# Four of eleven weight sums moved from the up projections to the first projections of a hybrid encoder block

## The chip, the cores and the metric

The kernel runs on one core of one Trainium2 chip. The metric is the device time of one execution in microseconds; lower is better. The core's engines are TensorE (PE, its weight loads PEld), VectorE (DVE), ScalarE (ACT), GpSimd (POOL) and SyncE (SP, which here only issues DMAs).

## The reference

One encoder block for 512 tokens of width 1024, all in float32:

```python
h = rms_norm(x, mix_norm_g)
proj = h @ w_in                      # mLSTM q,k,v,o,gates | NA q,k,v | memory q | merge gates
y_ml = mlstm_branch(...)             # bidirectional, chunkwise
y_na = neighbourhood_attention(...)  # 8 heads, 8 x 16 windows with bias
y_xa = memory_cross_attention(...)   # into rms_norm(mem)
merged = g_ml * (y_ml @ w_br_ml) + g_na * (y_na @ w_br_na) + g_xa * (y_xa @ w_br_xa)
x = x + merged @ w_out
a, u = split(rms_norm(x, ffn_norm_g) @ w_ffn_up)           # 1024 -> 2 x 2816
x = x + (gelu(dwconv3(a, w_conv, b_conv)) * u) @ w_ffn_down  # 2816 -> 1024
return rms_norm(x, final_norm_g)
```

The change concerns `w_ffn_down` (2816 x 1024) alone.

## The kernel before, in words

*Arithmetic.* A float32 product is made as three matmuls of rounded parts (`mm3`, lines 224 to 226): high x high, high x low, low x high. Each operand is therefore split: ACT writes the high part with a copy that rounds (line 184 for weights, 230 for activations), DVE subtracts it from the source for the low part (185, 231).

*Weights.* The weights of all projections lie in one array of blocks in the order of use (`BLOCKS`): four blocks `mlq`, four `mlk`, eight `tm` (values and gates, token-major), then `xaq`, `o`, `memk`, `memv`, `naq`, `nak`, gates and branches, and last 22 pairs `ua`, `uu` of the up projections. `weights(key)` is called where a block is first needed. It starts the DMA of blocks up to three ahead (`emit_raw`, line 160, on SP's queue, three buffers) and the split of the next one (`emit_split`, in halves, four buffers each for high and low parts). `BINDEX` gives a block's number; `mlk` 0 is 4, `xaq` 0 is 16.

*The down projection* is done by a Winograd-like scheme: its input and its weight are cut into 2 x 2 quarters, and seven products of sums of quarters (`ORDER`: p1, p5, p6, p3, p7, p2, p4) take the place of eight. The sums of the weight's quarters are made ahead of time, tile by tile (11 tiles of 128 rows, `HF`), and stored to DRAM: `tdn` holds two plain sums, `tsp` two sums already split into high and low. One tile is one sum of this text:

- `sum_load(k)`: 1 MB of the four quarters from `wdn` into a shared buffer (`unit`), DMA on POOL's queue (line 1477)
- first step: DVE adds two pairs of quarters (1495)
- `high`: takes a second shared buffer, DVE adds (1483), ACT writes the high parts (1484)
- `store`: DVE adds (1492), POOL issues the store to `tdn` (1493)
- `low`: DVE writes the low parts (1487), POOL issues two stores to `tsp` (1489)

The steps stand in the list `down_sums`, in the order first step, `high`, `store`, `low`. In the up projections, loop variable f from 0 to 21, iteration f loads the sum that `SUMS` names for it, and from f = 4 on takes up to three steps from the list:

```python
SUMS = [2 + 4 * k // 3 for k in range(HF)]
...
        if f in SUMS:
            sum_load(SUMS.index(f))
        if f >= 4:
            for _ in range(3):
                if down_sums:
                    down_sums.pop(0)()
```

*Order and buffers.* The program is traced in this order and then list-scheduled: on each engine and queue an instruction that is ready goes first by its place in the trace, with readiness as estimated at compile time. On the chip each engine works its list in order. `tc.issue_after(ins)` keeps instructions behind `ins` on the engine of `ins`. `unit` is a pool of 15 buffers of 128 x 2112 words, shared by operands, activations, heads' work and the sums.

*The first projections.* For `mlq`, eight steps over the input's k tiles are made with four banks at once, while x still arrives. `mlk` 0 and 1 follow, with two banks of another pool, begun earlier. During `mlk` 0 the token norm is made (`x_norm`: `rstd_wide`, lines 347 to 351, gives `rb_x`; `rstd_cols`, 337 and 340, gives `rc_x`). Then the convolutions evacuate the six banks (line 468 multiplies a bank by `rb_x` into `pad`, 470 to 472 convolve, 476 is the SiLU). `mlk` 2 needs the first of the four `mlq` banks back. The `tm` blocks follow; line 538 stores values to `nav_d` through POOL's queue.

Of the kernel before, what the change touches and what calls it, by code (L numbers as in the profile page):

```python
# [11 lines left out]
F32 = mybir.dt.float32  # L12
F32R = mybir.dt.float32r
AF = mybir.ActivationFunctionType
ALU = mybir.AluOpType
# [3 lines left out]
S = 512  # L19
# [6 lines left out]
HF = FT // 2  # L26
# [63 lines left out]
BINDEX = {}  # L90
# [12 lines left out]
def hybrid_block(ctx, tc, xg, xT, xtok, memT, wflat, wout, wdn, vecs, gbias, nabias, out):  # L103
    nc = tc.nc
    V, A, G, PE, SY = nc.vector, nc.scalar, nc.gpsimd, nc.tensor, nc.sync
# [13 lines left out]
    def nm(s):  # L119
        uid[0] += 1  # L120
        return f"{s}_{uid[0]}"

    def unit(dt=F32):
        return up.tile([P, UNIT], dt, tag="unit", name=nm("u"))
# [15 lines left out]
    B11, B12, B22, B21 = range(4)  # L140
    T1, T4, T3, T2 = range(4)
    GROUPS = ((0, 4), (4, 8), (8, HF))
    tdn = dp.tile([2, P, HF * S], F32, name="tdn")
    tsp = dp.tile([2, 2, P, HF * S], F32R, name="tsp")
# [4 lines left out]
    st = {"raw": 0, "split": 0, "last": BINDEX[("ua", 0)][0] - 1}  # L149

    def emit_raw(i):
        key, n = BLOCKS[i]
        _, off, _ = BINDEX[key]
        r = wp.tile([P, BW], F32, tag="raw", name=nm("wr"), bufs=3)
        raws[i] = r
        if i < 2:
            return [(r[:, a:b], wflat[off + P * a:off + P * b].rearrange("(p n) -> p n", p=P))
                    for a, b in zip(CUTS[i], CUTS[i][1:])]
        src = wflat[off:off + P * n].rearrange("(p n) -> p n", p=P)
        st["sy"] = SY.dma_start(r[:, :n], src).ins  # L160
# [7 lines left out]
    def emit_split(i):  # L168
        key, n = BLOCKS[i]
        r = raws.pop(i)  # L170
        c, hs = halves(i)
        split[i] = []
        for a, b in hs:
            m = (b - a) * c
            h = wp.tile([P, HWT], F32R, tag="hi", name=nm("wh"), bufs=4)
            l = wp.tile([P, HWT], F32R, tag="lo", name=nm("wl"), bufs=4)
            if key[:2] == ("tm", 2):
                h = h[:, HI256:]
            for u, v in ((0, P), (P, 2 * P), (2 * P, m)) if i == 0 and a == 0 else ((0, m),):
                src = r[:, a * c + u:a * c + v]  # L180
                if i == 0 and u == 0:
                    st["wh1"] = V.tensor_copy(h[:, u:v], src).ins
                else:
                    A.activation(h[:, u:v], src, AF.Copy)  # L184
                V.tensor_tensor(l[:, u:v], src, h[:, u:v].bitcast(F32), op=ALU.subtract)  # L185
            for k in range(a, b):
                q = slice((k - a) * c, (k - a + 1) * c)
                split[i].append((h[:, q], l[:, q]))
# [4 lines left out]
    def ahead_to(raw, spl):  # L193

        while st["raw"] <= min(raw, st["last"]):
            emit_raw(st["raw"])
            st["raw"] += 1
        while st["split"] <= min(spl, st["last"]):
            emit_split(st["split"])
            st["split"] += 1  # L200

    def weights(key):

        i, _, n = BINDEX[key]
        calls[0] += i >= BINDEX[("naq", 0)][0]
        if calls[0] % 2 and sums:
            sums.pop(0)()
        ahead_to(i + RAW_AHEAD, i + SPLIT_AHEAD)
        return split.pop(i)

    def sum_ops():
        for dst, src, more in ((T1, wout[B11], B12), (T3, wout[B12], B22), (T2, tout[T1], B22), (T4, tout[T2], B21)):
            for add in (False, True):
                def one(d=tout[dst], s=wout[more] if add else src, add=add):
                    if add:
                        G.dma_start(d, s, accum_op=ALU.add, max_dma_last_dim=4 * KT // 2 * S)
                    else:
                        with tc.issue_after(st["sy"]):
                            SY.dma_start(d, s)

                yield one

    def mm3(ps, lh, ll, rh, rl, start, stop):
        PE.matmul(ps, lh, rh, start=start, stop=False)  # L224
        PE.matmul(ps, lh, rl, start=False, stop=False)  # L225
        st["mm"] = PE.matmul(ps, ll, rh, start=False, stop=stop).ins  # L226
# [178 lines left out]
    def proj(key, XHs, XLs, n=S, at={}, ps=None):  # L405

        ws = weights(key)
        k0 = 0 if ps is None else 1
        if ps is None:
            ps = mmps()  # L410
        for k in range(k0, KT):
            mm3(ps[:, :n], ws[k][0], ws[k][1], XHs[k], XLs[k], k == 0, k == KT - 1)
            if k in (1, 3, 5):
                flush()
            if k in at:
                at[k]()
        return ps
# [3 lines left out]
    for k in range(KT):  # L421
        if k % 2 == 0:
            ws = weights(("mlq", k // 2))
        while done < min(KT, k + 1 + (k > 2)):
            x_part(done)
            done += 1
        wh, wl = ws[k % 2]
        if k == 1:

            for w, x in ((wh, XH), (wh, XL), (wl, XH)):  # L430
                for f in range(4):
                    PE.matmul(ps_q[f], w[:, f * P:(f + 1) * P], x[1], start=False, stop=False)  # L432
            continue
        for f in range(4):
            fs = slice(f * P, (f + 1) * P)
            if k == 0 and f == 0:
                hs = (slice(0, S // 2), slice(S // 2, S))
                for h in hs:
                    x_low(h)
                for i, (w, x, j) in enumerate(((wh, XH, 0), (wl, XH, 0), (wh, XH, 1), (wl, XH, 1), (wh, XL, 0), (wh, XL, 1))):  # L440
                    PE.matmul(ps_q[0][:, hs[j]], w[:, fs], x[0][:, hs[j]], start=i == 0, stop=False)
                continue
            mm3(ps_q[f], wh[:, fs], wl[:, fs], XH[k], XL[k], k == 0, k == KT - 1)
        if k == 0:
            ku = unit(F32R)
            kh, kl = ku[:, :2 * P], ku[:, S:S + 2 * P]
            split_act(kh, kl, wk)
            for f in range(2):
                fs = slice(f * P, (f + 1) * P)
                mm3(ps_k[f], kh[:, fs], kl[:, fs], XH[0], XL[0], True, False)  # L450
# [59 lines left out]
    for c in range(3):  # L510
        n, nk = TMC[c], TMK[c]
# [730 lines left out]

    gens = []
    so_ = list(sum_ops())
    sums.extend([so_[0], so_[2], so_[1], so_[3]] + so_[4:])

# [60 lines left out]
    for f in range(4):  # L1307
        ps = paced(("naq", f), RN)
        V.tensor_tensor(nq[:, f * S:(f + 1) * S].rearrange("p (b r c) -> p b r c", r=ROWS, b=4), rv(ps), rv(rb),
                        op=ALU.mult)  # L1310
# [15 lines left out]
    for br in range(3):  # L1326
# [19 lines left out]
        for fp in range(4):  # L1346
# [16 lines left out]
            for i in range(2):  # L1363
                f = 2 * fp + i
                ps = mmps()
                for k in range(4):
                    ks, fs = slice(k * S, (k + 1) * S), slice(i * P, (i + 1) * P)
# [71 lines left out]
    for n, name in enumerate(ORDER_O):  # L1439
        obank[name] = wide()  # L1440
        for k in range(4):
# [18 lines left out]
            for t in range(2):  # L1460
                q = slice(k * HS + t * P, k * HS + (t + 1) * P)
# [5 lines left out]
    for t in range(2):  # L1467
        normed(2 + t)


    down_sums = []

    def sum_load(k):
        w = unit()[:, :4 * S]
        w4 = w.rearrange("p (q n) -> p q n", q=4)
        ks = slice(k * S, (k + 1) * S)
        G.dma_start(w4, wdn[:, :, ks].rearrange("q p n -> p q n"))
        q = [w[:, i * S:(i + 1) * S] for i in range(4)]
        hl = []

        def high():
            hl.append(unit(F32R)[:, :4 * S].rearrange("p (x q n) -> p x q n", x=2, q=2))
            V.tensor_tensor(q[B22], q[B22], q[B11], op=ALU.add)
            A.activation(hl[0][:, 0], w4[:, 1:3], AF.Copy)  # L1484

        def low():
            V.tensor_tensor(hl[0][:, 1], w4[:, 1:3], hl[0][:, 0].bitcast(F32), op=ALU.subtract)
            for x in range(2):
                G.dma_start(tsp[:, x, :, ks].rearrange("q p n -> p q n"), hl[0][:, x])  # L1489

        def store():
            V.tensor_tensor(q[B21], q[B21], q[B22], op=ALU.add)
            G.dma_start(tdn[:, :, ks].rearrange("q p n -> p q n"), w4[:, 0:4:3])

        down_sums.extend([lambda: V.tensor_tensor(w[:, :2 * S], w[:, S:3 * S], w[:, :2 * S], op=ALU.add), high, store, low])


    PRODUCTS = {"p1": (wdn, B11), "p5": (tdn, 0), "p6": (tsp, 1), "p3": (wdn, B22), "p7": (tsp, 0), "p2": (wdn, B21),
                "p4": (tdn, 1)}
    TILES = [(n, k) for n in ORDER for k in range(HF)]  # L1500
# [51 lines left out]
            ops[name, g] = operand(name, quarters(g), GROUPS[g][1] - GROUPS[g][0])  # L1552
            ahead["op"] += 1

    SUMS = [2 + 4 * k // 3 for k in range(HF)]
    for f in range(FT):
        i, j = divmod(f, HF)
        if j % 4 == 0:
# [22 lines left out]
        V.tensor_tensor(ur, pu, c, op=ALU.mult)  # L1581
# [3 lines that stand above are left out]
# [76 lines left out]
    x = xt[3]  # L1661
# [137 lines left out]
```

## Time and profile before

| | |
|---|---|
| median of 3 runs | 857.08 us (856.96 to 857.18) |
| the profiled execution's own time | 857.81 us |
| its span, first to last instruction | 856.0 us |
| mean granted TensorE clock | 0.998 |
| TensorE busy | 848.5 us, 4175 matmuls |
| first projections (`mlk` 0 to the last `tm`) | about 28 to 94 us of the span |
| up projections | about 500 to 740 us |
| sums: first load issued, last store issued | 504.8 us, 690.0 us |

The profile is of one execution. A matmul's row lasts longer than the distance to the next matmul's start, as matmuls overlap; so the count of matmuls in a stretch says more of TensorE's pace than the busy time does. In a group's row, "out<-in" are the program's names; in a timeline row, the bracket is the idle time of the engine just before it and what ended it; PEq, SPq and so on are the engines' sequencers.

### The profile page before, as it was taken

How to read it: one execution, taken by the hardware profiler on the slowest of the kernel's cores; microseconds unless marked ns; L12 is line 12 of the kernel's file. 1: busy time of each engine (PE TensorE's matmuls, PEld its weight loads, DVE VectorE, ACT ScalarE, POOL GpSimd, SP SyncE). 2: the span in 40 equal slices, each digit the busy share in tenths (PEclk: the TensorE clock that was granted, in tenths of full speed). 3: DMA queues.
4: the chain of work that ended last, by engine and by line, in shares of the span. 5: the costliest groups of instructions: out<-in, count | busy, mean ns of one | idle time of the engine just before them, and what ended most of it. 6: DMA issues, size and time to landing. Idle time of an engine off the chain costs nothing.

```text
span 856.0 us, 12111 instructions
## 1 busy us (share of the span) xinstructions
PE 848.5 (99%) x4175; PEld 717.3 (84%) x4175; DVE 622.5 (73%) x1277; ACT 481.2 (56%) x989; POOL 133.0 (16%) x245
## 2 busy tenths in 40 slices
PE   9999999999999999999999999999999999999996
PEld 7898889988888888888888888888888888888885
DVE  7774698987568758898769967475758666694684
ACT  7663467675446658888735764343444444463463
POOL 0101100010127561600000111030213100011101
PEclk9999999999999999999999999999999999999999
DMA  7233542495674444543452844487869672477942
GB/s 281 80 111 121 185 153 85 158 281 163 179 202 120 115 125 127 158 144 128 144 186 98 225 144 156 153 293 261 265 222 348 208 231 99 135 258 258 380 161 100
DMA packets 53982, 155.00 MB, mean 181 GB/s; under 512 B 6872, under 2 KB 11992, under 8 KB 53344
## 3 DMA queue, kind: packets, MB, share of 16 engines
q1 hardware_dynamic: 30912, 101.37, 34.5%
q0 software_dynamic: 22576, 52.46, 20.8%
q8 instruction: 33, 0.54, 0.3%
q10 hardware_dynamic: 432, 0.39, 0.1%
q14 instruction: 29, 0.24, 0.1%
HBM read 132.68 MB, written 29.90 MB: 190 GB/s over the span
## 4 chain that ended last, share of the span: by engine, by line
PE 99%; DVE 0%; ACT 0%; POOLq 0%; issue 0%
PE mm L224 25%; PE mm L225 25%; PE mm L226 25%; PE at L225 6%; PE at L224 6%; PE at L226 6%; PE at L990 1%; PE at L971 1%; PE at L952 0%; PE at L953 0%; PE at L773 0%; PE at L821 0%; PE at L1078 0%; PE at L253 0%; PE mm L432 0%; PE mm L846 0%
## 5 line engine op out<-in xcount | busy, mean ns | idle before, releaser
L224 PE MATMUL mm<-u,wh 128*128 128x512 f32 (+1 forms) x859 | 330.2, 385 | 0.1
L225 PE MATMUL mm<-u,wh 128*128 128x512 f32 (+1 forms) x859 | 327.8, 382 | 0.0
L226 PE MATMUL mm<-u,wl 128*128 128x512 f32 (+1 forms) x859 | 327.7, 382 | 0.0
L184 ACT ACTIVATE wh<-wr 128x512 fp32r<-128x512 f32 (+2 forms) x240 | 149.7, 628 | 233.9 <-PE mm L225 199.8
L185 DVE TENSOR_TENSOR wl<-wr,wh 128x512 fp32r<-128x512 f32 (+2 forms) x242 | 164.1, 683 | 85.5 <-ACT wh L184 85.0
L226 PEld LDWEIGHTS mm<-u,wl 128*128 128x128 f32 x859 | 161.4, 188 | 31.5
L225 PEld LDWEIGHTS mm<-u,wh 128*128 128x128 f32 x859 | 161.6, 188 | 30.3 <-DVE u L231 0.4
L224 PEld LDWEIGHTS mm<-u,wh 128*128 128x128 f32 x859 | 161.4, 188 | 30.2 <-ACT u L230 0.4
L548 POOL DMA_DIRECT2D u<-nav_d x128 | 62.8, 534 | 56.2 <-PE at L990 23.4
L1132 ACT ACTIVATE u<-u 128x1024 fp32r<-128x1024 f32 (+1 forms) x28 | 27.5, 998 | 32.6 <-PE mm L226 9.0
L225 PE MATMUL at<-wl,u 128*128 128x512 f32 (+2 forms) x130 | 44.0, 339 | 0.0
L226 PE MATMUL at<-wh,u 128*128 128x512 f32 (+2 forms) x130 | 43.8, 337 | 0.0
L224 PE MATMUL at<-wh,u 128*128 128x512 f32 (+2 forms) x130 | 43.7, 337 | 0.0
L1134 DVE TENSOR_TENSOR u<-u,u 128x1024 fp32r<-128x1024 f32 (+1 forms) x21 | 23.7, 1134 | 13.6 <-ACT u L1132 13.5
L1581 DVE TENSOR_TENSOR u<-mm,s 128x512 f32<-128x512 f32 x22 | 15.2, 690 | 25.1 <-PE mm L226 23.6
L225 PE MATMUL mm<-wl,u 128*128 128x512 f32 x80 | 31.5, 394 | 0.0
L224 PE MATMUL at<-u,u 128*128 128x512 f32 x80 | 31.2, 390 | 0.0
L226 PE MATMUL mm<-wh,u 128*128 128x512 f32 x80 | 31.2, 390 | 0.0
L226 PE MATMUL at<-u,u 128*128 128x512 f32 x80 | 31.1, 389 | 0.0
L225 PE MATMUL at<-u,u 128*128 128x512 f32 x80 | 31.1, 389 | 0.0
L224 PE MATMUL mm<-wh,u 128*128 128x512 f32 x80 | 31.0, 390 | 0.0
L1489 POOL DMA_DIRECT2D tsp<-u x22 | 15.6, 709 | 96.7 <-ACT u L1484 90.1
(366 smaller groups left out, 1335.2 us busy)
## 6 DMA issues: line engine op xcount, KB each, us to landing
wr<-wflat SPq DMA_DIRECT2D x117, 512.0 KB, 3.6
u<-wdn POOLq DMA_DIRECT2D x11, 1024.0 KB, 8.2
tsp<-u POOLq DMA_DIRECT2D x22, 512.0 KB, 6.7
u<-tsp POOLq DMA_DIRECT2D x10, 1024.0 KB, 6.0
tdn<-u POOLq DMA_DIRECT2D x11, 512.0 KB, 5.7
tout<-wout POOLq DMA_DIRECT2D x4, 1024.0 KB, 10.2
nab<-nabias SPq DMA_DIRECT2D x16, 256.0 KB, 2.8
u<-nav_d POOLq DMA_DIRECT2D x128, 32.0 KB, 2.7
```

The lines of the kernel that those rows point to most:

```text
L184: A.activation(h[:, u:v], src, AF.Copy)
L185: V.tensor_tensor(l[:, u:v], src, h[:, u:v].bitcast(F32), op=ALU.subtract)
L224: PE.matmul(ps, lh, rh, start=start, stop=False)
L225: PE.matmul(ps, lh, rl, start=False, stop=False)
L226: st["mm"] = PE.matmul(ps, ll, rh, start=False, stop=stop).ins
L548: G.dma_start(vw[r * 32:(r + 1) * 32, i * 256:(i + 1) * 256], nav_v[hf, r, CW[b]:CW[b] + 32, hp * 256:(hp + 1) * 256])
L971: PE.transpose(pt[:, j * P:(j + 1) * P], sm[:, j * P:(j + 1) * P], ident)
L990: PE.matmul(py[:, bl * 256:(bl + 1) * 256], vw[:, c:c + P], pp[bl][:, hf * 256:(hf + 1) * 256], start=hf == 0, stop=hf == 1)
L1132: st["oh"] = A.activation(r3(h), src, AF.Copy, scale=scale).ins
L1134: V.tensor_tensor(r3(l), src, r3(h).bitcast(F32), op=ALU.subtract)
L1489: G.dma_start(tsp[:, x, :, ks].rearrange("q p n -> p q n"), hl[0][:, x])
L1581: V.tensor_tensor(ur, pu, c, op=ALU.mult)
```

## The change

`sum_load` and its list move ahead of the first projections in the trace. Sums 0 to 3 are loaded from `weights` when blocks `mlk` 0, `mlk` 3, `tm` (0, 1) and `tm` (1, 1) are asked for; these loads go to SP's queue, behind the weight block started last. On each later call for a block before `xaq` 0, two steps of the list are taken. The seven sums left are loaded in the up projections at f = 4, 6, 8, ... 16, on POOL's queue as before.

```diff
@@ weights(key)
         ahead_to(i + RAW_AHEAD, i + SPLIT_AHEAD)
+        if i < BINDEX[("xaq", 0)][0]:
+            for fn in down_sums[:2]:
+                down_sums.pop(0)()
+            if i in EARLY:
+                sum_load(EARLY[i], True)
         return split.pop(i)
@@
+    down_sums = []
+
+    def sum_load(k, tied=False):
+        w = unit()[:, :4 * S]
+        w4 = w.rearrange("p (q n) -> p q n", q=4)
+        ks = slice(k * S, (k + 1) * S)
+        src = wdn[:, :, ks].rearrange("q p n -> p q n")
+        if tied:
+            with tc.issue_after(st["sy"]):
+                SY.dma_start(w4, src)
+        else:
+            G.dma_start(w4, src)
...
+        down_sums.extend([lambda: V.tensor_tensor(w[:, :2 * S], w[:, S:3 * S], w[:, :2 * S], op=ALU.add), high, store, low])
+
+    EARLY = {BINDEX[key][0]: k for k, key in enumerate((("mlk", 0), ("mlk", 3), ("tm", 0, 1), ("tm", 1, 1)))}
@@ before the up projections
-    down_sums = []
-
-    def sum_load(k):
...
-        G.dma_start(w4, wdn[:, :, ks].rearrange("q p n -> p q n"))
...
@@
-    SUMS = [2 + 4 * k // 3 for k in range(HF)]
+    SUMS = [None] * len(EARLY) + [4 + 2 * k for k in range(HF - len(EARLY))]
```

The three steps `high`, `low` and `store`, left out here, are the same before and after.

More of the change, by code (lines that the diff above doesn't have):

```diff
@@ L221, in sum_ops, with high, low, store @@
                 yield one
+    down_sums = []
[9 more added lines that the diff above has]
+            G.dma_start(w4, src)
+        q = [w[:, i * S:(i + 1) * S] for i in range(4)]
+        hl = []
+        def high():
+            hl.append(unit(F32R)[:, :4 * S].rearrange("p (x q n) -> p x q n", x=2, q=2))
+            V.tensor_tensor(q[B22], q[B22], q[B11], op=ALU.add)
+            A.activation(hl[0][:, 0], w4[:, 1:3], AF.Copy)
+        def low():
+            V.tensor_tensor(hl[0][:, 1], w4[:, 1:3], hl[0][:, 0].bitcast(F32), op=ALU.subtract)
+            for x in range(2):
+                G.dma_start(tsp[:, x, :, ks].rearrange("q p n -> p q n"), hl[0][:, x])
+        def store():
+            V.tensor_tensor(q[B21], q[B21], q[B22], op=ALU.add)
+            G.dma_start(tdn[:, :, ks].rearrange("q p n -> p q n"), w4[:, 0:4:3])
+        down_sums.extend([lambda: V.tensor_tensor(w[:, :2 * S], w[:, S:3 * S], w[:, :2 * S], op=ALU.add), high, store, low])
+    EARLY = {BINDEX[key][0]: k for k, key in enumerate((("mlk", 0), ("mlk", 3), ("tm", 0, 1), ("tm", 1, 1)))}
     def mm3(ps, lh, ll, rh, rl, start, stop):
@@ L1468, in hybrid_block @@
         normed(2 + t)
-    down_sums = []
-    def sum_load(k):
[L1474 to L1495, printed above, removed]
     PRODUCTS = {"p1": (wdn, B11), "p5": (tdn, 0), "p6": (tsp, 1), "p3": (wdn, B22), "p7": (tsp, 0), "p2": (wdn, B21),
```

## The prediction

> **What bounds the kernel now.** I read the page first (shares by engine, the slices, the chain that ended last), then a table by stretch, then what the engines waited for, then the timeline of the one place where the moved work looks tight.
>
> ```profile
> PE 848.5 (99%) x4175; PEld 717.3 (84%) x4175; DVE 622.5 (73%) x1277; ACT 481.2 (56%) x989; POOL 133.0 (16%) x245
> PE 99%; DVE 0%; ACT 0%; POOLq 0%; issue 0%
> PE at L253 <- PEq L1792: 0.8, 1, 0.8
> ```
>
> The first line is busy time per engine, the second the shares of the chain of waits, the third the whole answer to "whom did TensorE wait for": one wait of 0.8 us, at the start. TensorE is the chain. A busy matmul row can still hide a stall, since matmuls overlap, so the next table is read for counts as well as for busy time. Columns: stretch, its length, then busy us and (xinstructions) for PE, weight loads, DVE, ACT, POOL, then the clock, the DMA share and GB/s.
>
> ```profile
> 0.00:40.00 40.00, 39.22 (x173) 32.12 (x174) 29.17 (x58) 26.13 (x43) 4.62 (x25) 1.00 0.55 192
> 480.00:520.00 40.00, 39.82 (x233) 34.73 (x232) 30.76 (x48) 26.83 (x54) 4.17 (x6) 1.00 0.53 168
> 560.00:600.00 40.00, 40.00 (x178) 33.13 (x177) 27.77 (x39) 15.89 (x26) 8.68 (x12) 1.00 0.86 297
> 720.00:760.00 40.00, 40.00 (x178) 33.14 (x177) 29.48 (x39) 20.83 (x32) 0.71 (x1) 1.00 0.46 148
> 840.00:856.00 16.00, 9.46 (x59) 8.39 (x57) 5.67 (x12) 4.56 (x11) 2.26 (x5) 0.88 0.34 132
> 24.00:48.00 24.00, 24.00 (x108) 19.87 (x107) 18.81 (x37) 15.25 (x23) 2.67 (x8) 1.00 0.27 94
> 48.00:94.00 46.00, 46.00 (x294) 42.05 (x293) 24.86 (x65) 21.90 (x40) 3.40 (x6) 1.00 0.41 136
> ```
>
> TensorE is without work for 856.0 - 848.5 = 7.5 us. Of these 40 - 39.22 = 0.78 lie at the start, 40 - 39.82 = 0.18 around 500 us, and 16 - 9.46 = 6.54 in the tail; nothing is left for the rest. The rows 560 to 600 and 720 to 760 are the main reading: in the first the sums are in full work (POOL 12 instructions, DMA share 0.86), in the second they are over (POOL 1, DMA share 0.46), and TensorE runs 178 matmuls in both. So the sums beside the up projections cost TensorE nothing today.
>
> **The change, part by part.** What one sum costs, by its rows (count, then duration ns least/median/most):
>
> ```profile
> L1477 POOL DMA_DIRECT2D u<-wdn x11: 753/766/872, 504.8 to 660.9; - x11
> DMA to landing us min/median/max: 5.7/8.2/14.2
> L1495 DVE TENSOR_TENSOR u<-u x11: 1217/1220/1226, 524.5 to 683.7; 128x1024 f32<-128x1024 f32 x11
> L1483 DVE TENSOR_TENSOR u<-u x11: 681/684/692, 525.7 to 686.1; 128x512 f32<-128x512 f32 x11
> L1492 DVE TENSOR_TENSOR u<-u x11: 683/686/694, 527.5 to 687.9; 128x512 f32<-128x512 f32 x11
> L1484 ACT ACTIVATE u<-u x11: 1044/1045/1048, 559.1 to 686.9; 128x1024 fp32r<-128x1024 f32 x11
> L1487 DVE TENSOR_TENSOR u<-u,u x11: 1217/1224/1228, 560.1 to 688.5; 128x1024 fp32r<-128x1024 f32 x11
> L1489 POOL DMA_DIRECT2D tsp<-u x22: 699/707/720, 560.4 to 690.0; - x22
> L1493 POOL DMA_DIRECT2D tdn<-u x11: 712/715/727, 528.5 to 688.9; - x11
> ```
>
> The second line is the time from issue to landing of the 1 MB load in the first. One sum takes DVE 1.220 + 0.684 + 0.686 + 1.224 = 3.81 us, ACT 1.05 us, and POOL 0.77 for the load and 0.715 + 2 x 0.707 = 2.13 for three stores.
>
> *Removed beside the up projections:* four sums, 15.3 us of DVE, 4.2 of ACT, 11.6 of POOL, four loads and twelve stores. By the equal 178 this is worth 0 on TensorE. What the sums hide behind is TensorE's own pace; nothing waits next.
>
> *Added beside the first projections:* the same 15.3 us of DVE and 4.2 of ACT, 8.5 us of POOL, and four loads that now stand on SP's queue, each behind a weight block. Room by the rows: DVE is idle 24 - 18.81 = 5.2 us between 24 and 48, and 46 - 24.86 = 21.1 us between 48 and 94. The first sum (3.8 us) and the other three (11.4 us) fit into these; ACT has 8.8 and 24.1 us free against 1.05 and 3.1. Cost on TensorE 0, provided the order inside leaves the urgent work in front. The cover is the lead of the weight splits and of the banks over TensorE; without cover each us of DVE would be a us of the end, 15.3 in all.
>
> *The place where that is tight* is the reciprocal root rb_x, since the first evacuations wait for it and the third mlk block needs their banks:
>
> ```profile
> 23.87 0.33 SPq L160 DMA_DIRECT2D wr<-wflat  x1
> 28.59 0.69 DVE L185 TENSOR_TENSOR wl<-wr,wh 128x512 fp32r<-128x512 f32 x1 [1.99 <-ACT wh L184]
> 30.68 0.69 DVE L185 TENSOR_TENSOR wl<-wr,wh 128x512 fp32r<-128x512 f32 x1 [1.40 <-ACT wh L184]
> 31.82 0.69 DVE L349 SCALAR_TENSOR_TENSOR s<-at,s 128x512 f32<-128x512 f32 x1 [0.46 <-ACT s L348]
> 33.45 0.69 DVE L351 SCALAR_TENSOR_TENSOR rb_x<-s,s 128x512 f32<-128x512 f32 x1
> 35.08 1.28 DVE L468 TENSOR_TENSOR pad<-mm,rb_x 128x512 f32<-128x512 f32 x2
> 37.70 0.39 PE L224 MATMUL mm<-u,wh 128*128 128x512 f32 x1
> ```
>
> The first of the two L468 ends near 35.08 + 1.28/2 = 35.7; TensorE takes that bank at 37.70. The lead is 2.0 us. Sum 0 is first called for in the middle of this: its load is issued behind the weight block of 23.87, so near 24.2, and its first two additions (1.22 + 0.68 = 1.90 us of DVE) are traced ahead of the pads. If they go into the free 1.40 and 0.46 us they push the pad by 1.90 - 0.46 = 1.4 us at most, inside the lead of 2.0. The third and fourth steps of sum 0 are traced behind all these evacuations. So I take 0; the other end stands under the rivals.
>
> *Queues passed.* The load moves from POOL to SP; SP issues in order, so a load that found no free buffer would hold the weight blocks behind it. SP's issue is 0.33 us by the row of 23.87, 1.3 for four. What is behind has a long lead:
>
> ```profile
> 29.31 0.33 SPq L160 DMA_DIRECT2D wr<-wflat  x1
> DMA to landing us min/median/max: 3.1/3.3/4.3
> 42.09 0.64 ACT L184 ACTIVATE wh<-wr 128x544 fp32r<-128x544 f32 x1
> GB/s 111 264 332 409 394 238 177 13 157 93 85 169 10 142 29 170 3 0 274 62 168 13 160 75 93 168 172 211 130 305 210 300 178 12 252 84 92 204 289 100
> ```
>
> The block issued at 29.31 lands near 32.6 (second line: the weight loads between 24 and 94 us) and is first read at 42.09, 9.5 us later. The last row is the rate in 40 slices of the first 125 us; at its best, 409 GB/s, 1 MB takes 2.6 us. A block pushed back by a whole sum load still has 6.9 us left. Of the 15 shared buffers the first projections hold about nine (four of x, qT, kT, two of mem, one of values) and each sum two, so two sums in flight make 13 and three make 15: enough, as long as the stores drain. POOL's stores wait for DVE and ACT; behind them on POOL stand only the nav_d stores near 80 us, which are read far later. Cost 0; with a blocked SP, the bound is the excess of the block over 6.9 us.
>
> *The seven sums that stay* are loaded at f = 4, 6, ... 16 instead of about every 1.33 blocks from f = 2, and since no backlog builds up, the addition now follows its load in the same f instead of two blocks later. That is a new wait for DVE: up to 14.2 us by the longest landing. The cover is the lead of the splits:
>
> ```profile
> DVE u L1495 <- DMA u<-wdn: 3.3, 2, 1.8
> 536.75 0.63 ACT L184 ACTIVATE wh<-wr 128x512 fp32r<-128x512 f32 x1 [1.56 <-PE mm L225]
> 539.47 0.63 ACT L184 ACTIVATE wh<-wr 128x512 fp32r<-128x512 f32 x1 [2.09 <-PE mm L225]
> 540.14 0.69 DVE L185 TENSOR_TENSOR wl<-wr,wh 128x512 fp32r<-128x512 f32 x1 [1.80 <-ACT wh L184]
> ```
>
> ACT waits for TensorE to free one of four half-block buffers, every 2.72 us; a buffer is filled three halves ahead, 8.2 us, less 0.63 and 0.69 and the hand-overs: a lead of some 6.7 us. Today two of the eleven additions waited, 1.8 us at most. I take 0; the upper end is 14.2 - 6.7 = 7.5 us for one sum that meets the slowest landing with nothing in between.
>
> **Sum.** 0 (removed) + 0 (added) + 0 (order in the rest). The profiled execution took 857.81 us, 856.0 of it span and 1.8 around it; the median of the runs shown is 857.08, 0.7 less. The forecast in terms of the median is 857.1.
>
> **Rivals.**
>
> 1. *Slower, at rb_x.* DVE, in order, reaches the first addition of sum 0 before its load has landed, and the chain of rb_x stands behind. From the addition on DVE has 1.22 + 0.68 + (35.7 - 30.68 - 0.46 = 4.6) = 6.5 us to the end of the first pad, which must be there by 37.70. It decides from a landing later than 31.2 us. Landings: issue 24.2 plus 5.7 / 8.2 / 14.2 is 29.9 / 32.4 / 38.4; two weight blocks' worth behind one on the same queue (3.3 + 2.6) gives 30.1. TensorE would stop for 0 / 1.2 / 7.2 us: 857.1, 858.3 or 864.3, some 860 for a case in between. For it: DVE is busy 18.81 of the 24 us there. Against: the early stretch moves only 94 GB/s and the 8.2 comes from a stretch at 297.
>
> 2. *Slower, in the up projections.* If each of seven additions stood right behind a load of 8.2 us, 8.2 - 6.7 = 1.5 us each, 10.5 in all: 867.6. Against: 1.8 us is the longest such wait now.
>
> 3. *The load doesn't start where it is put.* A fourth sum finds no buffer, SP is blocked, and a weight block comes late: it needs over 6.9 us of blocking to show; 8 to 10 us of it would cost 1 to 3, so 858 to 860.
>
> 4. *Faster.* If the sums hold TensorE back within its busy time, taking four out frees some of it. Weight loads fill 33.13 of 40 us in the up stretch; were all the other 6.87 stalls made by eleven sums, over the 185 us from the first load (504.8) to the last store (690.0) four of them would give 185 x 0.17 x 4/11 = 11.4 us: 845.7. The rows speak against it: 33.14 and 178 in the stretch that has no sums.
> The Trainium skill, page Perfetto Trace Analysis, section Identifying the Most-Contended Engine, says that matmul busy time is no good measure of what TensorE has left and that the share of weight loads is; by that rule 99% busy would leave some 16% to win here, by the equal rows nothing of it is the sums'. The trace does not bear out that headroom for this change.
>
> **How the numbers follow.** No change that counts: 0.80. Rival 1 by more than 1.7 us 0.08, rival 2 0.04, rival 3 0.04: slower 0.16. Rival 4, with whatever reordering gives elsewhere: faster 0.04, because outside start and tail only 0.18 us of TensorE is idle. 0.2% is 1.7 us, about what a measurement can tell here. The range runs from 856.0, a us of drift between runs and all of the small gaps won, to 859.5, the middle of rivals 1 and 3; it leaves out about 0.04 below and 0.11 above.
>
> **What would show it.** Right: TensorE again without idle time from 24 to 94 us and from 520 to 800, 178 matmuls per 40 us in the up projections, DVE about 15 us busier before 94 and as much less after 500, the first pads still done before 37.7. Rival 1: a gap of TensorE near 37.7 and DVE waiting for the wdn load near 30. Rival 2: DVE waits for wdn loads of over 6 us. Rival 3: an SP wait on the sum load and a late split between 60 and 80. The prediction is wrong if any step of the sums proves to sit ahead of urgent work, which the profile of before cannot show.

## The result, and the profile after

| | before | after |
|---|---|---|
| median of 10 runs each, same chip | 857.11 us (856.52 to 857.47) | 858.72 us (857.69 to 860.19) |
| ratio after to before | | 1.0021, 95% interval 1.0012 to 1.0031 |
| profiled execution, its span | 857.81, 856.0 us | 860.19, 858.4 us |

The change makes the kernel slower by about 1.6 us. The time lies in the predicted range, but not at the likeliest case: zero was forecast, and the interval excludes zero. (The largest chance was given to "no change that counts", within 1.7 us; 1.6 lies just inside it.) The profiled execution of after is the slowest of its ten; a second profile of each kernel, taken later on one chip, had spans of 857.3 (after) and 855.0 us (before). The budget below uses that second pair and takes from the first only what both show.

First the page's line of busy time and the whole list of waits of TensorE, both of after. Before had one wait, the 0.8 at the start.

```profile
PE 849.0 (99%) x4175; PEld 717.7 (84%) x4175; DVE 622.1 (72%) x1277; ACT 480.6 (56%) x989; POOL 130.3 (15%) x241
```

```profile
PE mm L263 <- DVE wl L185: 1.1, 1, 1.1
PE at L291 <- PEq L1802: 0.8, 1, 0.8
PE mm L262 <- ACT wh L184: 0.6, 1, 0.6
```

The work is the same (4175 matmuls, DVE 622 us). Two waits of TensorE are new, and both end at a weight split. The table by stretch says where they are; columns as in the prediction's table. After:

```profile
24.00:94.00 70.00, 68.26 (x380) 59.62 (x379) 55.56 (x112) 38.41 (x65) 14.21 (x25) 1.00 0.77 258
48.00:60.00 12.00, 11.35 (x86) 10.94 (x85) 11.97 (x19) 7.13 (x12) 0.00 (x0) 1.00 0.57 202
60.00:70.00 10.00, 10.00 (x53) 8.65 (x53) 8.94 (x20) 7.11 (x12) 3.62 (x5) 1.00 1.08 372
70.00:80.00 10.00, 8.91 (x39) 7.05 (x38) 4.55 (x15) 1.26 (x2) 0.72 (x1) 1.00 0.91 313
560.00:600.00 40.00, 40.00 (x178) 33.12 (x177) 23.37 (x33) 15.35 (x24) 5.79 (x8) 1.00 0.65 223
720.00:760.00 40.00, 40.00 (x178) 33.10 (x178) 29.42 (x40) 19.53 (x31) 0.00 (x0) 1.00 0.49 151
```

Before, the three stretches that matter:

```profile
48.00:60.00 12.00, 12.00 (x96) 11.88 (x95) 9.09 (x17) 7.02 (x12) 0.00 (x0) 1.00 0.36 124
60.00:70.00 10.00, 10.00 (x48) 8.35 (x48) 6.02 (x25) 4.54 (x8) 0.00 (x0) 1.00 0.29 99
70.00:80.00 10.00, 10.00 (x46) 8.29 (x45) 3.36 (x6) 3.49 (x7) 0.00 (x0) 1.00 0.23 73
```

TensorE loses 0.65 us of busy time between 48 and 60 and 1.09 between 70 and 80, which is all that is missing between 24 and 94 (70.00 - 68.26). In the up projections the count is again 178 per 40 us, with sums and without. What changed around the stops: DVE went from 9.09 to 11.97 of 12 us, and the memory traffic from 99 and 73 to 372 and 313 GB/s.

**Stop 1**, at 52.3 us. Timeline rows of after: TensorE's around the stop, ACT's and DVE's just before it.

```profile
52.17 0.29 PE L264 MATMUL at<-wh,u 128*128 128x272 f32 x1
52.30 0.28 PE L262 MATMUL at<-wh,u 128*128 128x272 f32 x1
53.23 0.50 PE L262 MATMUL mm<-wh,u 128*128 128x512 f32 x1 [0.65 <-ACT wh L184]
...
52.54 0.63 ACT L184 ACTIVATE wh<-wr 128x512 fp32r<-128x512 f32 x1 [0.46 <-PE at L264]
...
48.01 0.71 DVE L185 TENSOR_TENSOR wl<-wr,wh 128x544 fp32r<-128x544 f32 x1
51.94 0.71 DVE L185 TENSOR_TENSOR wl<-wr,wh 128x544 fp32r<-128x544 f32 x1
```

These matmuls follow each other by 0.13 us; the one at 53.23 was due at 52.43, so 0.80 us is lost. It is a matmul of the next block (bank `mm`, 512 columns), placed between those of the current block (`at`, 272 columns). It needs the high split that ACT starts only at 52.54, and ACT had waited for a buffer that TensorE freed with the matmul of 52.17. So TensorE's list asks for a split whose buffer the matmul two places ahead still holds. In before, that block's first matmul stands behind all the `at` ones, and the same two low splits stand earlier, as a pair:

```profile
60.59 0.40 PE L224 MATMUL mm<-wh,u 128*128 128x512 f32 x1
45.41 1.35 DVE L185 TENSOR_TENSOR wl<-wr,wh 128x544 fp32r<-128x544 f32 x2
```

The order is made at compile time. With four more DVE operations per sum in the list, the low splits come later (48.01 and 51.94 against 45.41); a likely reading, not shown, is that the scheduler filled the time so expected with a matmul that on the chip was not ready.

**Stop 2**, at 78.2 us. Timeline rows of TensorE, DVE and SP, then the landing times of the four early loads (least, median, most).

```profile
78.19 0.39 PE L262 MATMUL mm<-wh,u 128*128 128x512 f32 x1
79.67 0.50 PE L263 MATMUL mm<-wl,u 128*128 128x512 f32 x1 [1.09 <-DVE wl L185]
...
77.78 1.23 DVE L257 TENSOR_TENSOR u<-u 128x1024 f32<-128x1024 f32 x1 [5.18 <-DMA u<-wdn]
78.92 1.29 DVE L185 TENSOR_TENSOR wl<-wr,wh 128x512 fp32r<-128x512 f32 x2
...
64.20 1.27 SPq L237 DMA_DIRECT2D u<-wdn  x1
```

```profile
DMA to landing us min/median/max: 5.6/6.8/13.6
```

The matmul due at 78.42 starts at 79.67: 1.25 us. It waits for a low split, and DVE, which makes it, had stood idle for 5.18 us in front of the first addition of sum 3. That load was issued at 64.20 and landed 13.6 us later. DVE lost 5.18 + 1.23 us and TensorE 1.25 of it, so the low splits had a lead of some 5.2 us there. In the second trace of after the same wait cost TensorE 0.39 us; stop 1 was 0.80 again.

**Budget of the second pair** (857.3 - 855.0 = 2.3 us): 0.16 at the start, 0.82 between 44 and 56 (stop 1), 0.37 between 70 and 94 (stop 2), 0.76 between 780 and 842 (in the down projection), the rest near 0.2. The first pair shows 0.81, 1.39 and -0.35 in the three later places; so the last is not fixed by the program.

### The profile page after: what moved, and what is told of

The parts are those of the page before. It is cut to its first block, busy times and chain, and to the rows that moved or that the text cites. A ratio compares the mean times of both kernels' runs of the same rounds, so it can differ in the third digit from the quotient of the medians.

```text
span 858.4 us, 12104 instructions
## 1 busy us (share of the span) xinstructions
PE 849.0 (99%) x4175; PEld 717.7 (84%) x4175; DVE 622.1 (72%) x1277; ACT 480.6 (56%) x989; POOL 130.3 (15%) x241
## 4 chain that ended last, share of the span: by engine, by line
PE 96%; DMA 2%; DVE 1%; issue 0%; ACT 0%; POOLq 0%; ACTq 0%; SPq 0%
PE mm L263 25%; PE mm L262 25%; PE mm L264 24%; PE at L262 5%; PE at L263 5%; PE at L264 5%; DMA u<-wdn 2%; PE at L1028 1%; PE at L1009 1%; PE at L990 0%; PE at L991 0%; DVE wl L185 0%; PE at L811 0%; PE at L859 0%; PE at L1116 0%
## 5 line engine op out<-in xcount | busy, mean ns | idle before, releaser
L586 POOL DMA_DIRECT2D u<-nav_d x128 | 62.4, 514 | 52.3 <-PE at L1028 22.4
L1591 DVE TENSOR_TENSOR u<-mm,s 128x512 f32<-128x512 f32 x22 | 15.2, 692 | 28.1 <-PE mm L264 26.3
L1172 DVE TENSOR_TENSOR u<-u,u 128x1024 fp32r<-128x1024 f32 (+1 forms) x21 | 23.7, 1134 | 13.6 <-ACT u L1170 13.5
L262 PE MATMUL at<-u,u 128*128 128x512 f32 x80 | 31.2, 390 | 0.0
L264 PE MATMUL mm<-wh,u 128*128 128x512 f32 x80 | 31.2, 389 | 0.0
L255 POOL DMA_DIRECT2D tdn<-u x11 | 8.0, 724 | 140.5 <-DVE u L254 96.0
```

Of the source, the lines that this page charges most:

```text
L586: G.dma_start(vw[r * 32:(r + 1) * 32, i * 256:(i + 1) * 256], nav_v[hf, r, CW[b]:CW[b] + 32, hp * 256:(hp + 1) * 256])
L1172: V.tensor_tensor(r3(l), src, r3(h).bitcast(F32), op=ALU.subtract)
```

## The experiments

The letters in the expectations stand for the theories given there. The first four kernels ran together, beside 33 runs of before with a median of 857.28 us.

**e1: the steps follow their load by two and three weight blocks.**

```diff
-            for fn in down_sums[:2]:
-                down_sums.pop(0)()
+            for fn in due.pop(i, ()):
+                fn()
             if i in EARLY:
                 sum_load(EARLY[i], True)
+                due[i + 2], due[i + 3] = down_sums[:2], down_sums[2:]
+                down_sums.clear()
```

> The four early sums take their first two steps two weight blocks after the load instead of one, the last two steps three blocks after. Theory A (the loss is two stops of TensorE, some 0.8 us near 52 us from a pile-up on VectorE while the first sum falls between the convolutions, and 1.3 us near 78 us because VectorE stands in order behind the fourth load, which lands 13.6 us after its issue): the second stop goes, the first stays or shrinks, as the first sum's steps come later; 857.1 to 857.9. Rival B (VectorE has 15 us more to do in a stretch where it is nearly full, wherever the steps stand): 858.7 as in the changed kernel. Rival C (the transfer engines are full from 60 to 80 us, so the weight blocks themselves are late, 9.4 us for one of them): 858.5 or more, a stop near 78 us remains.

Measured 859.28 us (11 runs), ratio 1.0026 (1.0017 to 1.0035). In the trace TensorE doesn't stop between 24 and 94, and its last matmul stands at 849.1, against 849.2 in before's first trace (848.1 in its second, taken later). The expected 857.1 to 857.9 was still missed; against the first trace the time is found behind the last matmul. DMA issues of the last stretch, e1 and then before (median us from issue to landing in the last column):

```profile
q14 instruction: 2, 0.02, 0.3%
out<-u ACTq DMA_DIRECT2D x1, 256.0 KB, 3.7
```

```profile
out<-u ACTq DMA_DIRECT2D x1, 256.0 KB, 2.8
```

The last store of the output takes 3.7 us instead of 2.8, and a packet of an instruction queue falls into it, 1.9 us behind its issue (the row counts a second one, which comes after the store has landed). This was a new question, taken up with e7.

**e2: no DVE work in the four early sums.**

```diff
-            V.tensor_tensor(q[B22], q[B22], q[B11], op=ALU.add)
+            if not tied:
+                V.tensor_tensor(q[B22], q[B22], q[B11], op=ALU.add)
@@ low: ACT copies, DVE doesn't subtract; the same for the other two additions
+            if tied:
+                A.activation(hl[0][:, 1], w4[:, 1:3], AF.Copy)
```

> The early sums' loads and stores stay, and their work on VectorE is left out (three additions and the subtraction; ScalarE writes the low half with a second copy, so the four early tiles hold no sums). Theory A: both stops go, 856.9 to 857.4. Rival B: the same. Rival C: the blocks are as late as before, the stop near 78 us stays, 858.3 or more.

Measured 857.77 us, ratio 1.0008 (0.9999 to 1.0017), between the two expectations. Stop 1 is gone; the next block's first matmul is back at 60.48. Stop 2 isn't. Timeline rows of e2's ACT:

```profile
74.78 1.06 ACT L247 ACTIVATE u<-u 128x1024 fp32r<-128x1024 f32 x1 [6.57 <-DMA u<-wdn]
76.70 0.61 ACT L184 ACTIVATE wh<-wr 128x512 fp32r<-128x512 f32 x1
```

The first to read the load is now ACT, and ACT stands in front of it, 6.57 us, with a high split of a weight behind it and behind two copies of the sum. TensorE loses about 1.2 us at 76.6. So stop 2 doesn't come from how much DVE has to do: it belongs to whichever engine meets the late load in its list.

**e3: the arithmetic without its DMAs.** All eleven sums are made in the up projections as before; the early four run on a zeroed buffer.

```diff
-            with tc.issue_after(st["sy"]):
-                SY.dma_start(w4, src)
+            G.memset(w, 0.0)
@@ no stores of the early four
+    SUMS = [2 + 4 * k // 3 for k in range(HF)]
```

> All eleven sums beside the up projections, placed as before the change; beside the first projections the arithmetic of four sums runs in addition, on a buffer that GpSimd sets to zero, without load or store and with no use of the result. Theory A: no late load, so no stop near 78 us; the stop near 52 us of some 0.8 us can stay: 857.1 to 857.9. Rival B: 858.7. Rival C: 857.1. A rival D (the loss comes from the seven sums that stay, placed at every second f) expects 857.1 here as well, and 858.7 from the other three kernels.

Measured 858.49 us, ratio 1.0013 (1.0004 to 1.0021). This run was spoilt as a measurement of the time: the clearing of the first buffer went to the very start and slowed the first cast there (below, under the hardware), and the start took 1.8 us more than before's. Some 1.0 us of that are matmuls of 512 columns that follow each other by 0.43 us instead of 0.23; they go on to 8.5 us here and to 5.6 in before. Its trace can be used between 24 and 94: no stop of TensorE, with 57.25 us of DVE work against 55.56 in after. The DVE work alone, without the loads and in the list that came out here, does no harm.

**e4: three early sums, eight in the up projections.**

```diff
-    EARLY = {... (("mlk", 0), ("mlk", 3), ("tm", 0, 1), ("tm", 1, 1)))}
+    EARLY = {... (("mlk", 0), ("mlk", 3), ("tm", 0, 1)))}
```

> Three sums early instead of four, eight beside the up projections at f = 4 to 18. Theory A: the fourth load is the one that came late, so the stop near 78 us goes and the one near 52 us stays: 857.8 to 858.1. Rival B: three quarters of the loss, 858.3. Rival C: less traffic between 60 and 80 us, 857.5 to 858.0.

Measured 858.16 us, ratio 1.0009 (1.0000 to 1.0017). Stop 2 went with its sum; stop 1 stayed, in the same place and size. TensorE's timeline in e4:

```profile
51.82 0.28 PE L262 MATMUL at<-wh,u 128*128 128x272 f32 x1
52.75 0.50 PE L262 MATMUL mm<-wh,u 128*128 128x512 f32 x1 [0.65 <-ACT wh L184]
```

Due at 51.95, 0.80 us lost, again by a matmul of the next block among those of the current one. The two stops are thus two things.

The next four ran beside 7 runs of before with a median of 856.93 us: e5, and a second trace each of e1, after and before.

**e5: the lag of e1, and the loads spread to `mlk` 0, `tm` (0, 0), (1, 1), (2, 0).**

```diff
-        if i < BINDEX[("xaq", 0)][0]:
+        if i < BINDEX[("xaq", 2)][0]:
...
+    EARLY = {... (("mlk", 0), ("tm", 0, 0), ("tm", 1, 1), ("tm", 2, 0)))}
```

> Four early sums as in the version with the steps two blocks behind the load, and the loads moved further apart: mlk 0, tm (0, 0), tm (1, 1), tm (2, 0), where they were mlk 0, mlk 3, tm (0, 1), tm (1, 1). Theory A (stops of TensorE near 52 and 78 us from VectorE's order and from full transfer engines): no stop is left, no stretch of 20 us with the transfer engines full, 857.1 to 857.5. If the early sums cost for another reason that the traces so far do not show (theory E: something outside the first projections, in the start or the last store, that differs from program to program), the median stays near 859 though the trace has no stop.

Measured 867.77 us (4 runs), ratio 1.0127 (1.0110 to 1.0144). The expectation was missed by about ten. Waits of DVE and TensorE in e5, and DVE's row of the longest one:

```profile
DVE u L259 <- DMA u<-wdn: 15.4, 4, 7.2
PE mm L264 <- ACT wh L184: 2.0, 1, 2.0
```

```profile
94.10 1.23 DVE L259 TENSOR_TENSOR u<-u 128x1024 f32<-128x1024 f32 x1 [7.20 <-DMA u<-wdn]
```

DVE waited for all four loads, 15.4 us in sum, although the text puts two blocks between a load and its use. The last load was issued at 84.03 and landed 10.0 us later; the weight block issued behind it took 10.2. So a lag in the text isn't a lag on the chip: a step's place in the program's text is only its rank, and the scheduler, whose estimates are not on record, put the addition ahead of the landing. TensorE stopped at 77.35, 95.49, 98.06 and 124.55, and in between ran slowly for a time (below, under the hardware); together that is 7.5 of the 10.8 us, and the last store, 3.7 us again, adds 0.9.

**e1_again, after_again, before_again.**

> The version with the steps two blocks behind the load, once more, for a second trace: its median was 859.28, but its trace had no stop between 24 and 94 us and lost 1.2 us to before only behind the last matmul, where the last store landed after 3.7 us instead of 2.7. Theory A with stops that come and go from run to run: a stop of 0.5 to 2 us between 40 and 94 us in this trace. Theory E: no stop, and again a late last store or a slow start.

> The changed kernel once more, for a second trace. Theory A: the stop near 52 us is the same, since it is the order of the instructions; the stop near 78 us differs in size, since it hangs on a load's landing (13.6 us in the first trace), 0 to 1.5 us. Time 857.7 to 860.2.

> The kernel before once more, for a second trace: what start, stretches and the way from the last matmul to the end differ by between two runs of one program. No stop between 24 and 94 us under any theory; the start's stalls within 0.3 us of 0.56 and the last store's landing within 0.5 us of 2.7.

e1: 859.19 us, with the last store at 3.7 us again and a stop of 0.37 us at 82.8 that its first trace doesn't have. After: 859.02, stop 1 the same, stop 2 smaller, and one stop more, at 785 us. Before: 856.72. TensorE's rows in after_again:

```profile
785.26 0.39 PE L264 MATMUL mm<-u,u 128*128 128x512 f32 x1
786.15 0.47 PE L262 MATMUL mm<-u,u 128*128 128x512 f32 x1 [0.51 <-DMA u<-tsp]
```

The down projection waits for a load of split sums from `tsp` there; the loss is 0.66 us.

The next three ran beside 27 runs of before with a median of 857.18 us.

**e6: the traffic without the work.** The early four are loaded, and as many bytes are stored, but DVE and ACT do nothing on them.

```diff
+        def traffic():
+            first = G.dma_start(tdn[:, :, ks]..., w4[:, 0:4:3]).ins
+            with tc.issue_after(first):
+                for x in range(2):
+                    G.dma_start(tsp[:, x, :, ks]..., cz[0][:, :2 * S]...)
+        if tied:
+            down_sums.extend([zero, lambda: None, traffic, lambda: None])
+            return
```

> The transfers of the four early sums alone: the loads where the change has them, the store of two quarters as soon as the load has landed, and behind it the two 512 KB stores, from a buffer of zeros. Their arithmetic on VectorE and ScalarE is left out, so no engine that TensorE waits for stands behind a load; the four early tiles hold no sums. Theory A (VectorE or ScalarE in order behind a late load): no stop near 52 or 78 us, 857.0 to 857.5. Rival C (the weight blocks themselves are late in the full transfer engines): a stop of 0.5 to 1.5 us near 78 us stays, 857.8 to 858.8.

Measured 857.58 us, ratio 1.0003 (0.9994 to 1.0013): no difference from before. Two rows of e6, the stretch and POOL's wait for the loads:

```profile
24.00:94.00 70.00, 70.00 (x400) 61.92 (x399) 43.95 (x100) 37.00 (x62) 16.62 (x27) 1.00 0.80 271
```

```profile
POOL tdn L264 <- DMA u<-wdn: 54.9, 4, 28.1
```

The traffic is at least that of after (271 against 258 GB/s in the same stretch), weight blocks take up to 10.2 us to land (9.4 in after), and TensorE doesn't notice. The engine that stands in front of the loads is now POOL, for 54.9 us, and nothing urgent is behind it. This separates the rival that blamed late weight blocks from the theory of the engine standing in order: the first falls.

**e7: e1 with 17 idle instructions ahead of the up projections' second block** (7 on DVE, 9 on POOL, 1 on ACT), so that the instruction streams are shifted against the end.

```diff
+        if f == 1:
+            idle = tiny(3)
+            for _ in range(7):
+                V.memset(idle[:, 0:1], 0.0)
+            for _ in range(9):
+                G.memset(idle[:, 1:2], 0.0)
+            A.activation(idle[:, 2:3], vec[:, :1], AF.Copy)
```

> The version with the steps two blocks behind the load, with 7 idle instructions more on VectorE, 9 on GpSimd and one on ScalarE at f = 1 of the up projections, so that these engines have as many instructions as before the change. Theory F (in both traces of that version the last store lands after 3.7 us instead of 2.7 because a fetch of instructions falls 1.9 us behind its issue, and its place depends on how many instructions an engine has): the last store lands after 2.6 to 2.9 us again, and the median falls by about 1.0 us from 859.2 to 858.2. If the late landing has another cause: 859.2 and 3.7 us.

Measured 858.45 us, ratio 1.0016 (1.0007 to 1.0024), against e1's 1.0026. In its trace the last store lands after 2.8 us again and no instruction packet falls into it. e7's median is 0.8 us below e1's, about the 0.9 of the store, though the two intervals overlap; the trace shows the shorter end itself. TensorE has a stop of 0.46 us at 83.1 here, for a low split.

**e8: e7 with lags of three and four blocks; e9: e8 with the steps also held behind the low split made last on DVE.**

```diff
+                due[i + 3], due[i + 4] = down_sums[:2], down_sums[2:]
@@ e9 only; st["wl"] is the last low split of a weight that is traced
             for fn in due.pop(i, ()):
-                fn()
+                with tc.issue_after(st["wl"]):
+                    fn()
```

> As the version with idle instructions, and the first two steps of an early sum three weight blocks behind its load, the others four. Theory A: VectorE no longer finds a load under way, no stop between 24 and 94 us, and with theory F no late last store: 857.0 to 857.6, the same as before. If the waits for loads don't matter: 858.2 as the version with two blocks.

> As the version with the steps three blocks behind the load, and VectorE's instructions of these steps are held behind the low split of the weight block that is one ahead at that point. In the version before this one VectorE still stood 3.15 us in front of the third load at 72.4 us: the later place in the text is only a rank, and the list was written with the addition as early as the load was thought to land. Theory A: with the order forced VectorE waits for no early load, no stop between 24 and 94 us in this trace, and the median comes down from 858.1 to 857.0 to 857.5, the same as before. If the rest of 0.9 us is VectorE's fuller time or anything else outside the waits: 858.0.

e8: 858.09 us, ratio 1.0011 (1.0002 to 1.0020). e9, beside 15 runs of before with a median of 857.27: 858.35 us, ratio 1.0012 (1.0003 to 1.0021). Both missed their expectation. One row of e8's DVE, and the stretch:

```profile
72.39 1.23 DVE L259 TENSOR_TENSOR u<-u 128x1024 f32<-128x1024 f32 x1 [3.15 <-DMA u<-wdn]
```

```profile
48.00:60.00 12.00, 12.00 (x96) 11.88 (x95) 12.00 (x21) 7.54 (x14) 1.45 (x2) 1.00 0.62 191
```

DVE still waits 3.15 us in e8, but within the lead of the splits, so TensorE runs through; in e9 it doesn't wait for an early load at all. DVE is busy for 12.00 of the 12 us and TensorE has no stop, since its list has the next block's first matmul at 60.32. e8's profiled execution, the shortest of its eleven, has a span of 854.8 us, before_again's 855.0: without stops the change costs nothing in such a run. The medians remain 0.9 to 1.1 us above before. e9's trace (span 856.9) is late from the start (TensorE's 101st matmul begins at 24.14 us, against 23.64 and 23.37 in the two of before), loses some 0.6 us in short delays near 130 and 143 us, and has one stop, 0.5 us at 786, again by a `tsp` load. The landing of the two `tsp` loads issued between 770 and 773 us in e9:

```profile
DMA to landing us min/median/max: 8.6/9.5/10.4
```

The same pair in before:

```profile
DMA to landing us min/median/max: 5.7/6.6/7.6
```

In the traces without four loaded early sums (before, before_again, e3, e4) the slower of the two lands after 7.6 to 7.8 us; with four it takes 8.3 to 10.4 us in nine of ten traces, 7.7 in the tenth (e1_again). Stops near 785 us of 0.2 us and more are seen only there, but not in all of them. Before's first trace, too, loses 0.8 us against its second between 780 and 842, in short delays without such a stop. Why tiles stored 700 us earlier should be read more slowly was not tried, and it stays open. The start's spread is not the change's, as far as the traces go: that 101st matmul begins at 23.11 to 24.14 us in the ten with four loaded early sums, on both sides of before's two.

No kernel run here is faster than before.

## Why the prediction was right and wrong

*Removed beside the up projections: right.* 178 matmuls per 40 us with eleven sums, with seven and with none. This was read from counts in two stretches, and it also disposes of rival 4.

*The seven sums that stay: right.* DVE's waits for loads of sums in after, in us, times and the longest:

```profile
DVE u L257 <- DMA u<-wdn: 5.7, 2, 5.2
```

Both lie beside the first projections (0.56 at sum 0, 5.18 at sum 3); none is left for the up projections.

*The tight place at rb_x: right, and closely so.* Timeline rows of after:

```profile
30.16 1.23 DVE L257 TENSOR_TENSOR u<-u 128x1024 f32<-128x1024 f32 x1 [0.56 <-DMA u<-wdn]
36.00 1.28 DVE L506 TENSOR_TENSOR pad<-mm,rb_x 128x512 f32<-128x512 f32 x2
38.02 0.39 PE L262 MATMUL mm<-u,wh 128*128 128x512 f32 x1
```

Sum 0 landed 5.6 us after its issue at 24.57; rival 1 put the point of decision at 31.2, and 30.1 was its estimate for two blocks' worth behind one. The pads started 0.9 us later than before, and TensorE took the bank without a stop.

*Added beside the first projections: the step that failed.* The prediction set 15.3 us of DVE against 26.3 us of its idle time, by averages over 24 and 46 us, and took 0 "provided the order inside leaves the urgent work in front". The order didn't, and the prediction's own last sign came true: a step of the sums (sum 3's first addition) sat ahead of urgent work (a low split). Stop 1 (0.80 us) needs no lack of DVE time: e8 is fuller on DVE and runs through. It comes from TensorE's list, which the added work rearranged, and it stands in just the three traces (after, after_again, e4) in which a matmul of the next block is met at 52.8 to 53.2 us; in e1, e5 and e7 it stands at 54.7 to 55.4 and finds its operand ready, in the others behind 60. What part of the added work brings that list about is not isolated: it is gone without DVE's work (e2) and also without the DMAs (e3). No view of before could show this placement; the averages could not exclude it, and the term deserved an upper end of about a us rather than the bare 0.

*Queues passed: sized for one load alone.* The prediction took a 1 MB load at the best rate, 2.6 us, and gave the block behind it 6.9 us of spare time. The spare time was real, as e6 shows. But four loads, twelve stores and the weight blocks came together, and the step looked at what is behind the load on its queue, not at who waits for the load itself. SP's issue of the four loads took 0.43 to 1.27 us each, not the 0.33 of a weight block, with no harm seen. Landings of weight blocks issued between 60 and 82 us, after and then before:

```profile
DMA to landing us min/median/max: 3.3/6.1/9.4
```

```profile
DMA to landing us min/median/max: 3.1/3.2/3.3
```

The Trainium skill, page DMA: Bandwidth & Descriptors, section "Issuing engines are not separate DMA queues", says that DMAs started by different engines run on the same 16 DMA engines and interleave. The trace agrees: with stores from POOL and loads from SP together, a block's landing goes from 3.2 us to as much as 9.4, and sum 3's load takes 13.6.

*The rivals.* Rival 1's mechanism happened, at another sum: DVE in order in front of a load that hasn't landed, a low split behind it, at sum 3 and not at sum 0, for 0.4 to 1.25 us. It was worked out for the load that looked tight and not for the three that follow in fuller traffic. Rival 3 named the right stretch (a late split between 60 and 80) and the right time (858 to 860) by the wrong cause: the load started within the queue's order, and the late block was not what TensorE waited for. Rival 2 did not happen.

*The sum.* Stop 1 with 0.8 us is shown, by its trace rows and by its coming and going with the list's order; stop 2 with 0.4 to 1.25 us is shown, by its moving to ACT in e2 and its absence in e4 and e6. They make 1.2 to 2.05 us, around the 1.6 measured. That the versions without either stop aren't back at before's median says that the account isn't closed: some 0.9 us is unexplained in e8 and e9, and part of it may stand in after too. That 858.72 lies inside the range is partly luck: the forecast was 0 + 0 + 0, and the room above it was left for rivals 1 and 3, neither of which took place as written.

## What to carry to other kernels

Before moving work into an engine's idle time, read that time instruction by instruction: an in-order engine pays for the place of the work in its list, and a compile-time scheduler can rearrange the lists of other engines as well. A load that is used soon must be priced at its landing under all the traffic that the move itself makes, and its reader should be an engine with nothing urgent behind it. When the engine that sets the time has no gap at the place the work is taken from, as the equal counts showed, there is nothing to win, only something to lose.

## What the runs showed of the hardware

*A late instruction fetch can lengthen the end.* In three of the fourteen traces, both of e1 and that of e5, the output's last store landed 3.7 us after its issue, and in just these a packet of an instruction queue began 1.9 us behind that issue, while the store was under way. In the other eleven no such packet falls into the store, and it took 2.75 to 2.87 us. In after such packets come 0.9 us ahead of the store and 1.6 us after its landing; it took 2.9 us. 17 idle instructions, some 350 us earlier, moved the packet away in e7. How a single packet delays a store was not tried.

*TensorE fell to half pace after short stops.* e5's TensorE rows and stretches:

```profile
97.72 0.50 PE L264 MATMUL mm<-u,wh 128*128 128x512 f32 x1 [1.95 <-ACT wh L184]
100.07 0.63 PE L266 MATMUL mm<-u,wl 128*128 128x512 f32 x1
100.49 0.63 PE L264 MATMUL mm<-u,wh 128*128 128x512 f32 x1
100.00:110.00 10.00, 10.00 (x39) 8.09 (x38) 5.74 (x15) 3.26 (x7) 2.15 (x4) 0.85 1.12 335
```

After pauses of 1.95 and 0.61 us within 3.3 us, seven matmuls from 99.64 to 102.63 followed each other by 0.43 us instead of 0.23, and the granted clock of the stretch was 0.85. That added 7 x 0.2 = 1.4 us to the stops. The Trainium skill, page TensorE: Matmul & The Clock Gate, section "What's actually happening", says that the clock is halved after an idle window of about 3.4 us. The halved pace is what the row shows; the pauses were shorter than that window and not even in one piece.

*A clearing on POOL slowed DVE.* e3, and then the same cast in before:

```profile
2.48 1.80 POOL L236 MEMSET u<- 128x2048 f32 x1
3.46 0.90 DVE L182 CAST wh<-wr 128x128 fp32r<-128x128 f32 x1 [3.46 <-DMA wr<-wflat]
```

```profile
3.45 0.23 DVE L182 CAST wh<-wr 128x128 fp32r<-128x128 f32 x1 [3.45 <-DMA wr<-wflat]
```

The cast of 0.23 us took 0.90, and ended about when POOL's memset did (4.36 and 4.28 us). The three later clearings in e3 (39.7 to 45.1 us) did not lengthen DVE's work beside them: a low split took 0.68 us there, as in after.
